# The opening of a two-block transformer kernel: zeros on TensorE, one token half ahead, gate products in two parts

## Chip, cores and metric

One core of one Trainium2 chip. The metric is the device time of one execution in microseconds (µs), the median over several runs. The engines are TensorE (PE, products and transposes; its loads of the stationary operand are PEld), VectorE (DVE), ScalarE (ACT), GpSimd (POOL) and SyncE (SP, which here only issues DMAs).

## The reference

Two transformer blocks run one after the other on 256 tokens of width 1024. What matters here is the start of the first:

```python
u = rms_norm(h, norm_mix_g[l])
z = u @ w_in[l]
qa, ka, va, qk_b, vb, ob, ib, fb, ga, gb = jnp.split(z, IN_SPLITS, axis=-1)
...
i_pre = (ib + b_igate[l].astype(ib.dtype)).transpose(0, 2, 1)
f_pre = (fb + b_fgate[l].astype(fb.dtype)).transpose(0, 2, 1)
hb = mlstm_chunkwise(to_heads(qb, B_HEADS), to_heads(kb_, B_HEADS), to_heads(vb, B_HEADS), i_pre, f_pre)
```

The columns `ib` and `fb` of the input projection are the eight gates (four heads, two each) of a gated recurrence. After the mixers comes a feed-forward layer; the second block has two layers of feed-forward, attention, feed-forward.

## The kernel before

The 256 tokens are two halves, t = 0 and 1, of 128. A half lies in `h[t]` as 128 rows by 1024. For a projection it is turned over by eight transposes on PE (`flip`, L158, each against the identity in `cst`, four to a bank) and multiplied by the gains of the norm on DVE (`uf`, L385); the row's own factor 1/rms (`row_rstd`: a square with sum on ACT, `ms` on DVE, a power on POOL) is multiplied in later.

Each operand is then split in two parts of a four-byte format that PE takes at a quick pace (`fp32r`): a cast on ACT (`uh`, `wh`, L224) and the remainder on DVE (`ul`, `wl`, L225). A weight product is three products, wh·uh, wl·uh and wh·ul, each 128 by 128 by 512 columns (`mm3`, on L153). The weights stream through SP in pieces of 1 MB (`raw`, three buffers; the very first piece is loaded and split in halves), and a new piece is only issued when a buffer comes free.

What runs in which order on PE is written out by a small planner, `Order`: tasks yield either a wait in planned microseconds or events that have a due time, each PE instruction advances the planner's clock, and a task whose time has come puts its PE work there. The other engines' instructions are ordered by a scheduler from the data dependencies and the order of writing.

The opening is `first_mix`. `boundary` turns a half and splits it (planned waits 0 and 2.0 for the two halves). `lin_both` (L326) does the first 48 weight products, for two pieces and both halves. `recurrence` does the eight gate columns by `gate_mm`: 16 full-precision products of `wg` with `uf` (`uf,wg`, 8 by 128 columns, each two rows in the trace), both halves, then bias and arithmetic (`gT`, `gz`, `logf`). `constants` loads `c1`, `masks` and `mlg` and casts the masks (`caus`, `mlm`). `second_params` does small arithmetic for the second block (`pi`, `pf`, `ang`, `nt`, `trig`) whenever DVE has room.

Of the kernel before, what the change touches and what calls it, by code (L numbers as in the profile page):

```python
# [9 lines left out]
FR = mybir.dt.float32r  # L10
BF16 = mybir.dt.bfloat16
# [106 lines left out]
def kernel(  # L118
# [15 lines left out]
    nc = tc.nc  # L134
# [11 lines left out]
    def bank():  # L146
        return psg.tile([128, 512], F32, tag="g", name="bank")
# [4 lines left out]
    def mm(out, lhsT, rhs, start, stop):  # L152
        pe.matmul(out=out, lhsT=lhsT, rhs=rhs, start=start, stop=stop)  # L153
        n = rhs.free_size()
        side.now += n / 2400 if rhs.dtype != F32 else max(n, 128) / 600
# [20 lines left out]
    gc = base.tile([128, G_N], F32, name="gc")  # L176
    nc.scalar.dma_start(out=cst, in_=consts)
    nc.scalar.dma_start(out=gc, in_=cols)
    for t in range(2):
        for c in range(2):  # L180
            nc.sync.dma_start(out=h[t][:, 512 * c:512 * c + 512], in_=x[128 * t:128 * t + 128, 512 * c:512 * c + 512])
    ident = cst[:, C_ID:C_ID + 128]
    mhalf = base.tile([128, 16], F32, name="mhalf")
    pool.memset(mhalf, -0.5)
# [3 lines left out]
    def row_bcast(tile_, lo, n):  # L188
        nc.sync.dma_start(out=tile_, in_=rows[0:1, lo:lo + n].to_broadcast([128, n]))
# [19 lines left out]
    def load_to(n):  # L209
        while stream["load"] < min(n, NP):  # L210
            i = stream["load"]
            if i in kept:
                r = kept[i][0].tile([128, 2048], F32, tag="tx", bufs=2, name="rawx")
            else:
                r = wp.tile([128, 2048], F32, tag="raw", bufs=RAW_BUFS, name="raw")
            n_dma = 2 if i == 0 else 1
            for q in range(n_dma):
                w = 2048 // n_dma
                nc.sync.dma_start(out=r[:, w * q:w * q + w], in_=weights[piece_at.get(i, i), :, w * q:w * q + w])
            raws[i] = r  # L220
            stream["load"] += 1

    def split(hi, lo, src):
        c = act.copy(out=hi, in_=src)  # L224
        dve.tensor_tensor(out=lo, in0=src, in1=hi.bitcast(F32), op=ALU.subtract)  # L225
        return c
# [102 lines left out]
    def lin_both(us, pieces):  # L329

        accs = [bank() for _ in us]
        for a, i in enumerate(pieces):
            for m in range(2):
                for (uh, ul, ready), acc in zip(us, accs):
                    side.until(*ready)
                    wh, wl = half(i, m, 512)
                    for kk in range(2):
                        k = 4 * a + 2 * m + kk
                        mm3(acc, uh[:, k], ul[:, k], wh[:, kk], wl[:, kk], k == 0, k == 4 * len(pieces) - 1)
        return accs  # L340
# [33 lines left out]
    def put_T(u, k0, n, src, gains=None, gain1=None, keep=None):  # L374

        uh, ul, _ = u
        b = trbank()
        for i in range(n):
            flip(b[:, 128 * i:128 * i + 128], src[:, 128 * i:128 * i + 128])
        b3 = b.rearrange("p (k n) -> p k n", n=128)[:, 0:n]  # L380
        hi, lo = uh[:, k0:k0 + n], ul[:, k0:k0 + n]
        if gains is not None:
            s = tmp.tile([128, 4, 128], F32, tag="uf", bufs=4, name="uf") if keep is None else keep[:, k0:k0 + n]
            full[id(u[2]), k0] = s
            dve.tensor_tensor(out=s, in0=b3, op=ALU.mult,  # L385
                              in1=gains.unsqueeze(2).to_broadcast([128, n, 128]))
            split(hi, lo, s)
        elif gain1 is not None:
            act.activation(out=hi, in_=b3, func=AF.Copy, scale=gain1)
            dve.scalar_tensor_tensor(out=lo, in0=b3, scalar=gain1, in1=hi.bitcast(F32),  # L390
                                     op0=ALU.mult, op1=ALU.subtract)
        else:
            split(hi, lo, b3)

    def boundary(t, src, gains, wait=1.4, keep=None, after=None):

        u = new_u(t)
        ev = Ready()
        u[2].append(ev)

        def task():
            yield wait
            with crit():
                for c in range(2):
                    put_T(u, 4 * c, 4, src[:, 512 * c:512 * c + 512], gains=gains[:, 4 * c:4 * c + 4], keep=keep)
            side.ready(ev, 1.3)
            if after is not None:
                after()

        side.spawn(task())  # L410
        return u

    def gcol(lo):
        return gc[:, lo:lo + 8]
# [279 lines left out]
    def first_mix(p0):  # L694
        with tc.tile_pool(name="mix1", bufs=1, reuse_waits="tile") as mix:
            def big(name, shape=(128, 1024), dt=F32):
                return mix.tile(list(shape), dt, tag="c", bufs=C_BUFS, name=name)

            wg = mix.tile([128, 8, 8], F32, name="wg")
            nc.scalar.dma_start(out=wg, in_=w_gates)  # L700
            gbias = mix.tile([128, 8], F32, name="gbias")
            row_bcast(gbias, R_GATE, 8)
            identb = mix.tile([128, 128], BF16, name="identb")
# [3 lines left out]
            mlg = mix.tile([128, 512], F32, name="mlg")  # L707
            oh = mix.tile([128, 4, 128], F32, name="oh")

            def constants():  # L710
                nc.sync.dma_start(out=c1, in_=consts1[:, 0:512])
                masks = big("masks", (128, 256))
                nc.sync.dma_start(out=masks, in_=consts1[:, D_CAUS:D_CAUS + 256])
                row_bcast(mlg, R_MLG, 512)
                dve.tensor_copy(out=identb, in_=ident)
                dve.tensor_copy(out=caus, in_=masks[:, 0:128])
                dve.tensor_copy(out=mlm, in_=masks[:, 128:256])
                for i in range(4):
                    dve.tensor_copy(out=oh[0:4, i], in_=ident[0:4, i:i + 1].to_broadcast([4, 128]))

# [7 lines left out]
            u, r, rh = [], [], []  # L728
            gT = mix.tile([128, 256], F32, tag="th", bufs=2, name="gT")
            gz = mix.tile([128, 2, 8], F32, name="gz")  # L730
            uf = []
            for t in range(2):
                uf.append(big("uf", (128, 8, 128)))
                u.append(boundary(t, h[t], gcol(G_MIX1), 0.0 if t == 0 else 2.0, uf[t]))

            def gate_mm(t):
                gb = bank()
                for k in range(8):
                    mm(gb[0:8, 0:128], wg[:, k], uf[t][:, k], k == 0, k == 7)
                dve.tensor_copy(out=gT[0:8, 128 * t:128 * t + 128], in_=gb[0:8, 0:128])  # L740

            def gates0():
# [134 lines left out]
            def recurrence():  # L877
                for t in range(2):
                    yield u[t][2]
                    gate_mm(t)  # L880
                    r.append(row_rstd(h[t]))
                    rh.append(scaled(r[t], 0.5))
                yield 5.93
                constants()
                gates0()
                yield 0.69
                gates1()
                yield 13.34
                gates2()
                yield 0.83  # L890
                gates3()
                yield 1.87
                gates4()
                for hd in range(5):
                    if hd < 4:
                        yield [gates_ready, cv_ready[0, hd], cv_ready[1, hd]]
                        ml_scores(hd)
                        yield 2.92
                    if hd == 0:
                        yield V1_ready  # L900
                    if hd:
                        ml_out(hd - 1)
                for t in range(2):
                    yield [gob_ready[t]]
                    ml_norm(t)
                    yield 6.39
                    put_T(yT[t], 4, 4, yb[0][:, t])
                    side.ready(y_ready[t][2], 1.81)

            side.spawn(recurrence())  # L910


# [47 lines left out]
            def ev_conv(w):  # L960
                zr = [Ready(), Ready()]

                def convs():
                    yield zr
                    for bl in range(4):
                        conv(w, bl)
                        yield 7.62

                side.spawn(convs())

                def f(t, acc):
                    z = tmp.tile([128, 512], F32, tag="z", name="z")
                    act.activation(out=z, in_=acc, func=AF.Copy, scale=r[t])
                    if t == 0:
                        pool.memset(zT[w][:, :, 0:3], 0.0)

                    def task():
                        yield 1.18
                        act.copy(out=zT[w][:, :, 3 + 128 * t:131 + 128 * t], in_=flip4(z))
                        side.ready(zr[t], 0.57)  # L980

                    side.spawn(task())
                return f
# [654 lines left out]
```

## Time and profile before

| | |
|---|---|
| median of 3 runs | 1374.95 µs (1374.17 to 1375.53) |
| the profiled execution | 1374.35 µs |
| its span on the core | 1372.6 µs |
| PE busy | 1347.2 µs (98%) |
| DVE busy | 1106.1 µs (81%) |
| ACT busy | 853.4 µs (62%) |
| POOL busy | 90.4 µs (7%) |
| PE, first instruction | 3.99 µs from the span's start |
| PE, first weight product | 12.30 µs |

A profile is of one execution. Its span begins with the first instruction that the profiler records; the execution's own time is 1.75 µs longer. Times in the rows below are from the span's start. Busy PE is pipelined: the length of a row overlaps that of the next, so its pace is read from the distance between starts.

### The profile page before, as it was taken

The numbers are of one execution on the slowest core, as the hardware profiler recorded it, in microseconds if no ns is written. First come the engines' busy times: TensorE is split into PE (matmuls) and PEld (weight loads), VectorE is DVE, ScalarE is ACT, GpSimd is POOL, SyncE is SP. The second block draws the span as 40 slices with busy tenths as digits, with TensorE's granted clock in tenths as the row PEclk, the third lists the DMA queues.
The fourth block names the chain that finished last, engine by engine and source line by source line (L and its number), as shares of the span: only waits on it lengthen the run. The fifth ranks groups of instructions, "written<-read, shape, count | busy, mean of one in ns | idle before, by whom it ended". The sixth has DMA issues, their size and how long they took to land.

```text
span 1372.6 us, 17475 instructions
## 1 busy us (share of the span) xinstructions
PE 1347.2 (98%) x6418; PEld 1094.7 (80%) x6418; DVE 1106.1 (81%) x1624; ACT 853.4 (62%) x1327; POOL 90.4 (7%) x89
## 2 busy tenths in 40 slices
PE   8999999999999999999999999999999989999998
PEld 7777888888888888877788888888888767788887
DVE  8866579888789889767689888898897787698884
ACT  6656546665576666568666566666675658566662
POOL 0000000000010000022000000000010211000000
PEclk9999999999999999999999999999999989999999
DMA  8434564976577767463358766677675522567762
GB/s 304 155 115 152 194 227 154 307 237 192 186 255 222 219 254 230 169 216 128 106 211 281 225 229 215 251 220 219 261 215 180 184 99 98 189 196 260 268 188 88
DMA packets 41397, 278.00 MB, mean 203 GB/s; under 512 B 5216, under 2 KB 6240, under 8 KB 8544
## 3 DMA queue, kind: packets, MB, share of 16 engines
q1 hardware_dynamic: 35568, 243.09, 48.6%
q0 software_dynamic: 4320, 31.46, 11.3%
q10 hardware_dynamic: 1424, 2.34, 0.6%
q8 instruction: 50, 0.82, 0.2%
q14 instruction: 35, 0.29, 0.1%
HBM read 244.37 MB, written 1.05 MB: 179 GB/s over the span
## 4 chain that ended last, share of the span: by engine, by line
PE 90%; DVE 6%; POOL 1%; ACT 1%; issue 1%; DMA 0%; DVEq 0%; POOLq 0%; ACTq 0%
PE bank L153 85%; PE trbank L158 5%; DVE wl L225 2%; POOL fac L344 1%; DVE nm L654 1%; DVE ms L1156 0%; DVE z L1160 0%; DVE p L666 0%; ACT wh L224 0%; DVE p L652 0%; ACT p L656 0%; DMA cst<-in_consts_dram 0%; DVE z L1218 0%; DVE z L1220 0%; DVE h L1490 0%
## 5 line engine op out<-in xcount | busy, mean ns | idle before, releaser
L225 DVE TENSOR_TENSOR wl<-raw,wh 128x1024 fp32r<-128x1024 f32 (+1 forms) x548 | 522.0, 978 | 82.9 <-ACT wh L224 76.5
L224 ACT CAST wh<-raw 128x1024 fp32r<-128x1024 f32 (+1 forms) x548 | 454.9, 856 | 126.2 <-PE bank L153 118.4
L153 PE MATMUL bank<-wh,uh 128*128 128x512 f32 x948 | 383.1, 404 | 0.0
L153 PE MATMUL bank<-wh,ul 128*128 128x512 f32 x948 | 373.3, 394 | 0.5 <-DVE ul L225 0.5
L153 PE MATMUL bank<-wl,uh 128*128 128x512 f32 x948 | 372.8, 393 | 0.0
L153 PEld LDWEIGHTS bank<-wh,ul 128*128 128x128 f32 x948 | 179.0, 189 | 40.7 <-DVE ul L225 1.2
L153 PEld LDWEIGHTS bank<-wh,uh 128*128 128x128 f32 x948 | 179.3, 189 | 38.0 <-issue 2.0
L153 PEld LDWEIGHTS bank<-wl,uh 128*128 128x128 f32 x948 | 179.5, 189 | 35.0 <-DVE wl L225 0.3
L153 PE MATMUL bank<-wh,hh 128*128 128x512 f32 x440 | 174.3, 396 | 0.0
L153 PE MATMUL bank<-wl,hh 128*128 128x512 f32 x440 | 172.1, 391 | 0.3 <-DVE wl L225 0.3
L153 PE MATMUL bank<-wh,hl 128*128 128x512 f32 x440 | 172.2, 391 | 0.0
L224 ACT CAST wh<-tn 128x1024 fp32r<-128x1024 f32 x60 | 63.2, 1053 | 100.6 <-PE bank L153 54.4
L225 DVE TENSOR_TENSOR wl<-tn,wh 128x1024 fp32r<-128x1024 f32 x60 | 73.3, 1222 | 39.5 <-ACT wh L224 39.1
L153 PEld LDWEIGHTS bank<-wh,hl 128*128 128x128 f32 x440 | 82.6, 188 | 18.1
L153 PEld LDWEIGHTS bank<-wl,hh 128*128 128x128 f32 x440 | 82.7, 188 | 17.9 <-DVE wl L225 0.8
L153 PEld LDWEIGHTS bank<-wh,hh 128*128 128x128 f32 x440 | 82.7, 188 | 17.0
L153 PE MATMUL bank<-wh,sh 128*128 128x512 f32 x240 | 93.7, 390 | 0.0
L153 PE MATMUL bank<-wl,sh 128*128 128x512 f32 x240 | 93.7, 390 | 0.0
L153 PE MATMUL bank<-wh,sl 128*128 128x512 f32 x240 | 93.6, 390 | 0.0
L224 ACT CAST hh<-trbank 128x512 fp32r<-128x512 f32 (+1 forms) x60 | 33.0, 551 | 62.8 <-PE trbank L158 58.9
L225 DVE TENSOR_TENSOR wl<-rawx,wh 128x1024 fp32r<-128x1024 f32 x60 | 71.6, 1217 | 0.0
L224 ACT CAST wh<-rawx 128x1024 fp32r<-128x1024 f32 x60 | 63.0, 1054 | 13.3 <-PE bank L153 10.8
(248 smaller groups left out, 1533.3 us busy)
## 6 DMA issues: line engine op xcount, KB each, us to landing
raw<-in_weights_dram SPq DMA_DIRECT2D x196, 1024.0 KB, 5.0
rawx<-in_weights_dram SPq DMA_DIRECT2D x30, 1024.0 KB, 8.9
rawx<-rawx POOLq DMA_DIRECT2D x15, 1024.0 KB, 7.8
tn<-raw POOLq DMA_DIRECT2D x15, 1024.0 KB, 7.6
mem<-in_mem_dram ACTq DMA_DIRECT2D x4, 512.0 KB, 3.5
Tb<-in_rel_dram SPq DMA_DIRECT2D x3, 512.0 KB, 5.7
h<-in_x_dram SPq DMA_DIRECT2D x4, 256.0 KB, 3.8
raw<-in_weights_dram SPq DMA_DIRECT2D x2, 512.0 KB, 5.5
```

The source lines that it names most:

```text
L153: pe.matmul(out=out, lhsT=lhsT, rhs=rhs, start=start, stop=stop)
L158: pe.transpose(out=out, in_=in_, identity=ident if identity is None else identity)
L224: c = act.copy(out=hi, in_=src)
L225: dve.tensor_tensor(out=lo, in0=src, in1=hi.bitcast(F32), op=ALU.subtract)
L344: pool.tensor_tensor(out=dst, in0=src, in1=mhalf[:, 0:n], op=ALU.pow)
L654: dve.tensor_reduce(out=nm, in_=s, axis=AX.X, op=ALU.max, negate=True)
```

## The change

Zeros (seven products of 512 columns ahead of the first transposes, twelve behind) go onto PE. The first half of x is loaded ahead of the first weights, the second half behind the first half piece. `lin_both` does a whole piece for the first token half and then for the second, where it had changed over in mid-piece. The weight casts are ordered behind the first half's own casts. The gate products take the two-part operands: `wg` is split into `wgh` and `wgl`, and 3 × 8 products a half replace 8, placed 2.5 planned microseconds behind their operands. Loading the constants is split from using them, and two planned waits are longer.

```diff
+    load_x(0)
...
+                if i == 0 and q == 0:
+                    load_x(1)
...
-            for m in range(2):
-                for (uh, ul, ready), acc in zip(us, accs):
-                    side.until(*ready)
+            for (uh, ul, ready), acc in zip(us, accs):
+                side.until(*ready)
+                for m in range(2):
                     wh, wl = half(i, m, 512)
...
-                    put_T(u, 4 * c, 4, src[:, 512 * c:512 * c + 512], gains=gains[:, 4 * c:4 * c + 4], keep=keep)
+                    cast = put_T(u, 4 * c, 4, src[:, 512 * c:512 * c + 512], gains=gains[:, 4 * c:4 * c + 4], keep=keep)
+            if order[0] is None:
+
+                order[0] = cast
...
+            zeros = mix.tile([128, 512], BF16, name="zeros")
+            dve.memset(zeros, 0.0)
+
+            def idle_products(n):
+                b = bank()
+                for i in range(n):
+                    pe.matmul(out=b, lhsT=zeros[:, 0:128], rhs=zeros, start=True, stop=True)
+
...
-            uf = []
+            idle_products(7)
             for t in range(2):
-                uf.append(big("uf", (128, 8, 128)))
-                u.append(boundary(t, h[t], gcol(G_MIX1), 0.0 if t == 0 else 2.0, uf[t]))
+                u.append(boundary(t, h[t], gcol(G_MIX1), 0.0 if t == 0 else 3.4))
+
+            def filler():
+
+                yield 0.05
+                idle_products(12)
 
             def gate_mm(t):
                 gb = bank()
+                if t == 0:
+                    split(wgh, wgl, wg)
+                uh, ul, _ = u[t]
                 for k in range(8):
-                    mm(gb[0:8, 0:128], wg[:, k], uf[t][:, k], k == 0, k == 7)
+                    mm(gb[0:8, 0:128], wgh[:, k], uh[:, k], k == 0, False)
+                    mm(gb[0:8, 0:128], wgh[:, k], ul[:, k], False, False)
+                    mm(gb[0:8, 0:128], wgl[:, k], uh[:, k], False, k == 7)
                 dve.tensor_copy(out=gT[0:8, 128 * t:128 * t + 128], in_=gb[0:8, 0:128])
...
                     yield u[t][2]
+                    yield 2.5
                     gate_mm(t)
...
-                constants()
+                load_constants()
                 gates0()
                 yield 0.69
                 gates1()
+                constants()
...
+            side.spawn(filler())
             side.spawn(recurrence())
...
-                        yield 1.18
+                        yield 2.4
```

What PE gets at the head of the program stands first in the order of before (`h_75` and `h_76` are the two token halves):

```order
L158 MATMUL trbank<-cst,h_75 128x128 x8
L158 MATMUL trbank<-cst,h_76 128x128 x8
L153 MATMUL bank<-uf,wg 8x128 x16
L153 MATMUL bank<-wh,uh 128x512
L153 MATMUL bank<-wl,uh 128x512
L153 MATMUL bank<-wh,ul 128x512
```

and so in the order after the change, from behind the last zeros, with what each row waits for (a number behind an engine's name is only a mark):

```order
L153 MATMUL bank<-wh,uh 128x512 [waits Activation_49]
L153 MATMUL bank<-wl,uh 128x512 [waits DVE_49]
L153 MATMUL bank<-wh,ul 128x512
L158 MATMUL trbank<-cst,h_76 128x128 [waits DMAHW6_49,PE_49]
L158 MATMUL trbank<-cst,h_76 128x128 x3
L158 MATMUL trbank<-cst,h_76 128x128 [waits DMAHW7_49,PE_49]
L158 MATMUL trbank<-cst,h_76 128x128 x3
L153 MATMUL bank<-wh,uh 128x512 [waits Activation_49]
L153 MATMUL bank<-wl,uh 128x512 [waits DVE_49]
```

The transposes of the second half and all gate products moved behind the first weight products.

On DVE, from the last casts of the first half on, the order of before is this:

```order
L225 TENSOR_TENSOR ul<-uf,uh 128x512
L225 TENSOR_TENSOR ul<-uf,uh 128x512 [waits Activation_49]
L740 COPY gT<-bank 8x128 [waits PE_49]
L362 TENSOR_SCALAR rs<-r 128x1 [waits Pool_49]
L354 TENSOR_SCALAR ms<-ss 128x1
L225 TENSOR_TENSOR wl<-raw,wh 128x512 [waits DMAHW0_49,Activation_49]
L740 COPY gT<-bank 8x128 [waits PE_49]
L362 TENSOR_SCALAR rs<-r 128x1 [waits Pool_49]
L225 TENSOR_TENSOR wl<-raw,wh 128x512 [waits Activation_49]
```

After the change the rows from the first weight split on are these:

```order
L230 TENSOR_TENSOR wl<-raw,wh 128x512 [waits DMAHW4_49,Activation_49]
L230 TENSOR_TENSOR wl<-raw,wh 128x512 [waits Activation_49]
L359 TENSOR_SCALAR ms<-ss 128x1
L367 TENSOR_SCALAR rs<-r 128x1 [waits Pool_49]
L359 TENSOR_SCALAR ms<-ss 128x1 [waits Activation_49]
L390 TENSOR_TENSOR uf<-trbank,gc 128x512 [waits PE_49] x2
L230 TENSOR_TENSOR wl<-raw,wh 128x512 [waits DMAHW0_49,Activation_49]
L230 TENSOR_TENSOR ul<-uf,uh 128x512 [waits Activation_49] x2
L230 TENSOR_TENSOR wl<-raw,wh 128x512
```

The gain products of the second half (`uf`) and the wait for POOL (`rs`) stand between the splits of the first piece's two halves, and the gate copies (`gT`) are gone from there.

Further on, in DVE's order after the change, the casts of the masks have moved between the two halves of the fourth piece's split:

```order
L772 COPY gT<-bank 8x128 [waits PE_49]
L367 TENSOR_SCALAR rs<-r 128x1 [waits Pool_49]
L230 TENSOR_TENSOR wl<-raw,wh 128x512 [waits DMAHW4_49,Activation_49]
L230 TENSOR_TENSOR wl<-raw,wh 128x512 [waits Activation_49]
L772 COPY gT<-bank 8x128 [waits PE_49]
L739 CAST caus<-masks 128x128 [waits DMAHW0_49]
L740 CAST mlm<-masks 128x128
L230 TENSOR_TENSOR wl<-raw,wh 128x512 [waits Activation_49] x2
L230 TENSOR_TENSOR wl<-raw,wh 128x512 [waits DMAHW5_49,Activation_49]
L230 TENSOR_TENSOR wl<-raw,wh 128x512 [waits Activation_49]
L779 SCALAR_TENSOR_TENSOR gz<-trbank,r,gbias 128x8 [waits DMAHW3_49,PE_49]
```

Before, `caus` and `mlm` stood 51 rows behind the second `gT`, among the last of the gate arithmetic; the small parameter operations (`pf` to `trig`) that were in between have gone to the boundary of the feed-forward layer.

## Rows read from the trace of the kernel before

**Rows 1.** The page: busy time, share, instructions; the chain by line
```profile
PE 1347.2 (98%) x6418; PEld 1094.7 (80%) x6418; DVE 1106.1 (81%) x1624; ACT 853.4 (62%) x1327; POOL 90.4 (7%) x89
...
PE bank L153 85%; PE trbank L158 5%; DVE wl L225 2%; POOL fac L344 1%; DVE nm L654 1%; DVE ms L1156 0%; DVE z L1160 0%; DVE p L666 0%; ACT wh L224 0%; DVE p L652 0%; ACT p L656 0%; DMA cst<-in_consts_dram 0%; DVE z L1218 0%; DVE z L1220 0%; DVE h L1490 0%
```

**Rows 2.** What PE waited for, 0 to 100: us in total, times, longest
```profile
PE trbank L158 <- DMA cst<-in_consts_dram: 4.0, 1, 4.0
```

**Rows 3.** Timeline of PE, 0 to 25: start us, us, engine, line, operation
```profile
3.99 4.04 PE L158 MATMUL trbank<-cst,h 128*128 128x128 f32 x16 [3.99 <-DMA cst<-in_consts_dram]
7.96 4.42 PE L153 MATMUL bank<-uf,wg 128*8 128x128 f32 x32
12.30 0.50 PE L153 MATMUL bank<-wh,uh 128*128 128x512 f32 x1
...
16.04 0.39 PE L153 MATMUL bank<-wh,uh 128*128 128x512 f32 x1
...
18.09 0.39 PE L153 MATMUL bank<-wh,uh 128*128 128x512 f32 x1
...
24.48 0.39 PE L153 MATMUL bank<-wh,ul 128*128 128x512 f32 x1
```

**Rows 4.** The same in the stretch 8.5 to 9
```profile
8.13 1.27 PE L153 MATMUL bank<-uf,wg 128*8 128x128 f32 x5
```

**Rows 5.** The same in the stretch 11.5 to 12.8
```profile
11.34 1.04 PE L153 MATMUL bank<-uf,wg 128*8 128x128 f32 x8
```

**Rows 6.** The chain of waits, 0 to 30: start us, us, what
```profile
3.99 1.97 PE trbank L158 x8
...
25.56 0.87 PE trbank L158 x8
```

**Rows 7.** Timeline of ACT, 0 to 18
```profile
1.72 0.38 ACTq L700 DMA_DIRECT2D wg<-in_w_gates_dram  x1
...
5.62 0.19 ACT L350 ACTIVATION_READ_ACCUMULATOR junk<-h 128x1 f32 x1
...
10.02 2.23 ACT L224 CAST wh<-raw 128x512 fp32r<-128x512 f32 x4
```

**Rows 8.** DMA issues: KB each, median us from issue to landing
```profile
masks<-in_consts_dram SPq DMA_DIRECT2D x1, 128.0 KB, 5.8
...
wg<-in_w_gates_dram ACTq DMA_DIRECT2D x1, 32.0 KB, 4.4
```

**Rows 9.** Timeline of DVE, 0 to 21
```profile
6.00 0.69 DVE L385 TENSOR_TENSOR uf<-trbank,gc 128x512 f32<-128x512 f32 x1 [0.16 <-PE trbank L158]
...
12.68 1.87 DVE L225 TENSOR_TENSOR wl<-raw,wh 128x512 fp32r<-128x512 f32 x3
...
20.47 0.35 DVE L747 SCALAR_TENSOR_TENSOR gz<-trbank,r,gbias 128x8 f32<-128x8 f32 x2
```

**Rows 10.** Timeline of PE, 83 to 87 (128-column products of bf16)
```profile
83.93 0.28 PE L153 MATMUL bank<-caus,identb 128*128 128x128 bf16 x2
```

**Rows 11.** Timeline of PE, 44.5 to 48
```profile
46.39 0.23 PE L153 MATMUL bank<-mlm,identb 128*128 128x128 bf16 x1
```

**Rows 12.** Timeline of DVE, 21 to 34
```profile
24.65 0.19 DVE L1127 TENSOR_SCALAR nt<-nt 128x64 f32<-128x64 f32 x1
...
29.38 0.22 DVE L716 CAST caus<-masks 128x128 bf16<-128x128 f32 x1
...
30.59 0.16 DVE L771 SCALAR_TENSOR_TENSOR logf<-gz,pp 128x8 f32<-128x8 f32 x1
```

**Rows 13.** Timeline of SP, 0 to 30
```profile
21.44 0.42 SPq L713 DMA_DIRECT2D masks<-in_consts_dram  x1
```

**Rows 14.** DVE by stretch: busy us, granted clock, DMA share, GB/s
```profile
15.00:20.00 5.00, 4.90 (x12) 1.00 0.88 290
```

**Rows 15.** Timeline of DVE, 199 to 212
```profile
204.80 0.69 DVE L1077 SCALAR_TENSOR_TENSOR h<-bank,h 128x512 f32<-128x512 f32 x1 [2.82 <-PE bank L153]
```

**Rows 16.** What PE waited for, 100 to 1373
```profile
PE trbank L158 <- DVE p L1255: 3.8, 1, 3.8
```

## What the change will do: the prediction

> **What bounds the kernel now.** Times are µs from the span's start. I read the page first: PE is busy for 98% of the span and carries 85% + 5% of the chain on its two lines, the products (L153) and the transposes (L158) [rows 1]. So what counts is work that PE is given, or waits that PE gets, and hardly what the other engines do. Then I read what PE waited for: once in the first 100 µs, 4.0 for the constants in front of its first transpose [rows 2]. The timeline of PE gives the order of that opening: 16 transposes from 3.99, the gate products from 7.96, the first weight product at 12.30, and then one weight product after another [rows 3]. From 16.04 to 18.09 lie 9 of them, .228 each. The 51st starts at 24.48 and so ends at 24.71; the two gate transposes lie before it [rows 3].
>
> The pace of the opening is worth a look. In the middle of the gate products five rows take 1.27, so .21 to .25 lie between starts, by what is allowed for the length of the last; at the end eight take 1.04, in the same way .11 [rows 4, 5]. The eight transposes of a token half take 1.97 there and .87 later [rows 6]. PE's opening runs at half the later pace, which I read as the lower of its two clock levels (1.2 and 2.4 GHz).
>
> So the kernel's opening is 12.3 µs in which PE does no weight product, and everything behind it is a row of PE work without a hole. A change here is worth what it moves a fixed place in that row, and I take the end of the 51st weight product, 24.71.
>
> **The change part by part.** *An earlier first product.* The first token half no longer waits for the second. ACT's square of the first half ends at 5.81 [rows 7]; the gate weights, issued at 1.72 and 4.4 to landing, are there at 6.1 [rows 7, 8], so their short cast (new) ends at about 6.4. Two casts of u at .56 each (four casts of that size take 2.23 [rows 7]) end at 7.5 and the two of the first weight half at 8.6. DVE follows with the differences at .6 each (three take 1.87 [rows 9]): the first weight half is split by 8.8 and 9.4. On PE eight transposes end at 5.96 [rows 6], then come twelve products of zeros, the first at the half pace (.45, twice .228), the rest at .228: 6.0 + .45 + 11 × .228 = 8.95. The first weight product starts at about 8.95 in place of 12.30.
>
> *What comes right behind it.* Six weight products (1.37) end at 10.3, the second half's eight transposes (.87 at the full pace [rows 6]) at 11.2. The weights' next half then has to be split. On DVE the order puts two gain products for the second token half (uf) ahead of that: the first can start after four transposes, at about 10.75, the second ends at about 12.05 (.69 and a pitch of .6 [rows 9]), the split at 12.7. PE has only one product to run meanwhile, and stands for about 1.4 µs. I take 12.8 as the time when it runs on, with 7 of the 51 products done. From below it is 12.3 (ACT had cast the whole piece at 12.25 before [rows 7], the third of four .55 sooner, and .6 for a split); from above 13.3, one more split.
>
> *The gate products.* Before, 16 products (32 rows) lay ahead of 12.30, in time that PE spent waiting anyway. Now there are 48, all behind 12.8, in between weight products. No row of before has the two-part format at 128 columns. From below: two bf16 products of 128 columns take .28, a lone one .23, so .05 lies between starts [rows 10, 11]; a quarter of .228 is .057, and I put the lower end at .056. From above: .11, a row of the same 128 columns by 8 in the four-byte format [rows 5]. I take .08, between them, since this format runs at the quick pace at 512 columns but each product here loads a stationary operand of its own. 48 × .08 = 3.84 (2.7 to 5.3).
>
> The Trainium skill, "TensorE: Matmul & The Clock Gate", section "Back-to-back issue gap", gives about 81 ns for each pair of load and product at 128 columns; by that the term would be 3.9.
>
> *The sum of the opening.* From 12.8: 44 products × .228 = 10.0 and the gate products 3.84, so the 51st ends at 26.65. The two gate transposes, which lay ahead of it, now stand right behind it: .3, taken from the eight of .87 with some room for the change of bank. PE has done at 26.95 what it had done at 24.71: +2.2.
>
> *The masks.* Before, DVE used masks at 29.38 [rows 12], long after they had landed (issued at 21.44, 5.8 to landing [rows 8, 13], so 27.2). Now the two casts of masks stand behind the second gate copy, between the two halves of a weight piece's split. DVE gets there at about 21 and stands until the landing, 5 to 6 µs. Behind it wait the rest of that piece, all later ones, and the gate arithmetic (gz was at 20.47 [rows 9], now about 28.5). DVE has had hardly a free moment there, 4.90 of 5.00 [rows 14], but it also loses some 19 small parameter operations (each about .19 [rows 12], .13 between starts), 2.5 µs. So it falls behind by up to 3. PE needs the delayed half (of the fourth piece) 15 products and eight transposes after 26.95, at 31.2; DVE has it by 29. The gate chain took DVE from 20.47 to 30.75 (logf) [rows 9, 12], so it would end near 39; PE uses its result behind the 114th weight product, which by 12.8 + 107 × .228 + 3.84, with 16 transposes and the two of the gates, is near 43. That covers it by 4; without the cover the price is up to 2.5. I take .3.
>
> *The feed-forward boundary.* The small parameter operations now stand around the residual add (h) that started at 204.80 after 2.82 idle on DVE [rows 15]. Some 12 of them come before its second part, about 2 µs, so they fit into that idle time unless the positions, now loaded just ahead, are late; ACT also has a table load more. Nothing to 1.7; I take .5.
>
> *Free parts.* The earlier load of x and the split of load and use of the constants cost nothing that PE sees, since SP and the queue feed PE only through the splits above; the later convolution task moves a wait that PE does not have.
>
> Together 2.2 + .3 + .5 = +3.0 on the profiled execution's 1374.35, 1377.35. The median of the runs shown is 1374.95, .60 above it; with the same distance, **about 1378.0**.
>
> **The rivals.** *A, the gate products are cheap.* At .056 the term is 2.7, the opening +1.1, and with the masks and the boundary hidden, as the covers above allow, the kernel ends at 1374.95 + 1.1 to 1.9, 1376.0 to 1376.9. For it: the format's 512-column products take .228, one column in .44 ns, and the bf16 row has 128 columns at .05. Against it: 48 of them alternate with 48 loads. This would not be slower by more than .2%; it decides from a price of about .074 down.
>
> *B, 128 columns are slow in this format.* A four-byte gate product of before is two rows of .11; if a two-part product of so few columns got no better than that whole product, .22, the 48 take 10.5 and the sum is +9.6: 1384.6. For it: no product of this format here has fewer than 512 columns. Against it: it always shows one row, not two.
>
> *C, zeros do not raise the clock.* Twelve at .45 end at 11.4 instead of 8.95; all behind them on DVE moves by 2.4 (transposes, uf, split): 1380.4. For it: nothing in the profile shows zeros on PE, and before, PE kept the low level until well into the gate products, at 9 µs, after 5 µs of work [rows 3, 4]. Against it: it now starts work before 3.99, without a wait for a DMA.
>
> The section "What's actually happening" of the same page of the Trainium skill makes the clock rise with sustained activity of the array; by that the zeros serve, and C falls.
>
> *D, DVE's wait for masks reaches PE*, with the boundary's 1.7: +2.2 + 2.5 + 1.7, 1381.3. It decides if the gate chain ends over 4 µs later than I have it.
>
> *E, faster.* PE has waits elsewhere, the largest 3.8 [rows 16]. That one ends with DVE and lies where the order is the same, so I see no mechanism that would take 2.75 from it or the others; in the opening even at .056 and with the run-on at 12.3 the sum is +.6.
>
> **How the numbers follow.** .2% is 2.75 µs, about what a measurement of this kernel can tell from no change. The forecast (1377.0 to 1379.0) has a chance of .42, A .30, B .08, C .08, D .05, E .07. The range reaches down to 1374.0, below A's best, and up to 1382.0, above C and D: left out are B and most of E, under .2. Faster is E, .07. Slower (above 1377.7) are three quarters of the forecast, B, C and D: .32 + .21 = .53. The rest is the same, .40.
>
> **What would show it.** In the profile after: zeros on PE from about 1 and again from 6 at .23; the first weight product near 9; eight transposes of .87 behind the sixth; a wait of PE for a split (wl) of 1 to 2 ending near 12.8; 24 gate rows in about 1.9, twice; the 51st weight product's end near 27. DVE should stand for the masks until about 27 with no new wait of PE for the gate chain, and at the boundary (now near 208) PE should lose under 1. The prediction is wrong if the gate rows are .056 or .2 apart, if the wait near 12 is missing, if the first weight product is not before 10.5, or if a later wait of PE grows or vanishes by more than 1 µs.

## The result, and the profile after

The changed kernel takes 1382.28 µs (median of 4 runs, 1380.87 to 1383.85), the kernel before 1374.56 (4 runs, 1373.41 to 1375.53): a ratio of 1.0059, 95% interval 1.0045 to 1.0074. It is slower by 7.7 µs, where 3.0 were forecast. The profiled execution took 1382.28, and its span is 7.9 longer than that of before.

The page of the changed kernel, the span and the busy times:

```profile
span 1380.5 us, 17547 instructions
...
PE 1352.9 (98%) x6453; PEld 1097.1 (79%) x6453; DVE 1106.7 (80%) x1626; ACT 854.5 (62%) x1329; POOL 89.9 (7%) x89
```

Busy PE has grown by 5.7, its share is the same [rows 1]. So PE has more to do or does it more slowly, and where, the timeline of the opening tells. First ACT (start, length, operation, and in brackets the idle time before it and what ended it):

```profile
1.73 0.38 ACTq L717 DMA_DIRECT2D wg<-in_w_gates_dram  x1
...
7.79 0.24 ACT L229 CAST wgh<-wg 128x64 fp32r<-128x64 f32 x1 [1.91 <-DMA wg<-in_w_gates_dram]
7.94 1.13 ACT L229 CAST uh<-uf 128x512 fp32r<-128x512 f32 x2
```

The gate weights (wg) are asked for at 1.73 as before, but land at 7.77, after 6.04, where it was 4.4 [rows 8]. Their small cast (wgh) stands first in ACT's order, and ACT waits 1.91 for it. The casts of u stand behind: their input was ready at 5.7 to 6.3, and they start at 7.94. PE shows what comes of it:

```profile
4.15 1.19 PE L158 MATMUL trbank<-cst,h 128*128 128x128 f32 x8
5.18 2.75 PE L714 MATMUL bank<-zeros 128*128 128x512 bf16 x12
9.64 0.51 PE L153 MATMUL bank<-wh,uh 128*128 128x512 f32 x1 [1.71 <-ACT wh L229]
10.54 0.50 PE L153 MATMUL bank<-wl,uh 128*128 128x512 f32 x1 [0.39 <-DVE wl L230]
10.87 0.45 PE L153 MATMUL bank<-wh,ul 128*128 128x512 f32 x1
11.12 0.63 PE L153 MATMUL bank<-wh,uh 128*128 128x512 f32 x1
11.54 0.63 PE L153 MATMUL bank<-wl,uh 128*128 128x512 f32 x1
...
12.40 1.91 PE L158 MATMUL trbank<-cst,h 128*128 128x128 f32 x8
```

The twelve zeros behind the transposes end at 7.93, and the first weight product starts at 9.64. That is .7 later than I had it, after 1.71 of idle time, and the second waits another .39. Then the pace changes: .25 lie between the third product and the fourth, and .43 from there on; the eight transposes, ahead of the product at 13.96, take 1.6 in place of .87 [rows 6]. The view of stretches gives PE's busy time and, behind it, the granted clock, the DMA share and GB/s:

```profile
11.00:16.00 5.00, 4.00 (x15) 0.66 0.59 243
```

The granted clock fell: a mean of .66 from 11 to 16 (and .51 from 11 to 14, the level of 1.2 GHz). All of this is upstream of DVE's two gain products for the second token half (uf), and they stand ahead of the split (wl) that PE needs next:

```profile
13.49 0.69 DVE L390 TENSOR_TENSOR uf<-trbank,gc 128x512 f32<-128x512 f32 x1 [1.38 <-PE trbank L158]
...
14.95 0.68 DVE L230 TENSOR_TENSOR wl<-raw,wh 128x512 fp32r<-128x512 f32 x1
```

So PE goes on like this:

```profile
13.96 0.73 PE L153 MATMUL bank<-wh,uh 128*128 128x512 f32 x1
15.69 0.50 PE L153 MATMUL bank<-wl,uh 128*128 128x512 f32 x1 [1.00 <-DVE wl L230]
...
16.26 0.22 PE L153 MATMUL bank<-uh,wgh 128*8 128x128 f32 x1
...
17.69 0.45 PE L153 MATMUL bank<-wh,uh 128*128 128x512 f32 x1
```

PE runs on at 15.69, with 7 of the 51 products done, where I had 12.8. The gate products are the one thing that came out cheaper: 24 from 16.26 to 17.69, .060 each, 2.9 for the 48.

Further on PE has waits that were not there before [rows 2]. The view of what PE waited for in the first 100 µs (in total, times, longest):

```profile
...
PE trbank L158 <- DVE at L813: 1.0, 1, 1.0
PE trbank L158 <- DVE gz L779: 0.9, 1, 0.9
PE trbank L158 <- DVE z L1041: 0.6, 1, 0.6
PE trbank L158 <- DVE Mrow L820: 0.3, 1, 0.3
```

These four, 2.8 in all, are the ones behind the opening: gz, at and Mrow come between 30 and 55, and z at 88.84. DVE's timeline has the origin of the first three:

```profile
29.68 0.23 DVE L739 CAST caus<-masks 128x128 bf16<-128x128 f32 x1 [5.00 <-DMA masks<-in_consts_dram]
```

DVE stands for 5.00 in front of the first cast of the masks. PE's timeline around the gate transposes (28.95), and some of the transposes of z behind them:

```profile
28.95 0.29 PE L158 MATMUL trbank<-cst,gT 8*128 8x8 f32 x2
...
31.34 0.60 PE L158 MATMUL trbank<-cst,z 128*128 128x128 f32 x4
32.87 0.63 PE L158 MATMUL trbank<-cst,z 128*128 128x128 f32 x4 [0.92 <-DVE gz L779]
...
88.84 0.66 PE L158 MATMUL trbank<-cst,z 128*128 128x128 f32 x4 [0.61 <-DVE z L1041]
```

The second four of z need a bank that the gate arithmetic (gz) has not yet read, since gz stands behind the masks on DVE. At the gate transposes' end, 29.24, PE is 4.5 later than at 24.71 before. The idle time of the four waits adds 2.8, but they cost more. The profile counts idle time from the modelled end of the row before, and a row that does not wait starts earlier than that. By the distance between starts, the z of 88.84 begins 1.01 behind the product before it, and in the kernel before such a row begins .23 behind (80.66 and 80.89), so this wait costs .8 and not .6. In the same way gz costs 1.1, at 1.2 and Mrow .3. Together the four cost 3.4, and with the 4.5 that makes 7.9. A fixed place behind all of them, the products of qkT, is here in the kernel before:

```profile
109.60 0.70 PE L153 MATMUL bank<-qkT 64*128 64x256 f32 x4
```

and here in the changed kernel:

```profile
117.59 0.70 PE L153 MATMUL bank<-qkT 64*128 64x256 f32 x4
```

They are 8.0 later, and the end of the span is 7.9 later. So everything is lost before 110 µs, and the feed-forward boundary costs nothing.

### The profile page after: what moved, and what is told of

It reads as the page before. It is cut to its first block, busy times and chain, and to the rows that moved or that the text cites. A ratio compares the mean times of both kernels' runs of the same rounds, so it can differ in the third digit from the quotient of the medians.

```text
span 1380.5 us, 17547 instructions
## 1 busy us (share of the span) xinstructions
PE 1352.9 (98%) x6453; PEld 1097.1 (79%) x6453; DVE 1106.7 (80%) x1626; ACT 854.5 (62%) x1329; POOL 89.9 (7%) x89
## 3 DMA queue, kind: packets, MB, share of 16 engines
q0 software_dynamic: 4320, 31.46, 11.2%
## 4 chain that ended last, share of the span: by engine, by line
PE 87%; DVE 8%; ACT 1%; POOL 1%; issue 1%; DMA 1%; ACTq 0%; SPq 0%; DVEq 0%; POOLq 0%
PE bank L153 83%; PE trbank L158 4%; DVE wl L230 3%; POOL fac L349 1%; ACT wh L229 1%; DVE nm L662 1%; DMA masks<-in_consts_dram 0%; DMA wg<-in_w_gates_dram 0%; DVE cv L850 0%; DVE z L1195 0%; DVE p L674 0%; DVE p L660 0%; DVE ms L1191 0%; DVE ul L230 0%; DVE z L1253 0%
```

## The experiments

All were timed against the kernel before, on the same chip as their neighbours. The kernel before had medians of 1374.5 to 1375.3 in these groups, and its single runs lie within 1371.5 to 1377.7. The span is that of the one profiled execution.

| kernel | median µs | ratio to before, 95% interval | span µs |
|---|---|---|---|
| changed kernel | 1382.28 | 1.0059 (1.0045 to 1.0074) | 1380.5 |
| the same again (e11) | 1380.62 | 1.0041 (1.0026 to 1.0056) | 1379.4 |
| e1: masks later | 1378.32 | 1.0034 (1.0021 to 1.0047) | 1376.5 |
| e2: gate cast later | 1377.21 | 1.0024 (1.0012 to 1.0036) | 1376.3 |
| e3: both | 1375.38 | 1.0009 (1.0000 to 1.0019) | 1373.8 |
| e4: 20 zeros | 1379.74 | 1.0044 (1.0031 to 1.0056) | 1378.5 |
| e5: x first | 1380.77 | 1.0038 (1.0024 to 1.0053) | 1375.7 |
| e6: e3 without zeros | 1378.54 | 1.0028 (1.0017 to 1.0039) | 1377.8 |
| e7: before with 7 zeros | 1375.04 | 1.0005 (.9995 to 1.0014) | 1374.5 |
| e8: e3, transposes first | 1377.27 | 1.0013 (1.0004 to 1.0022) | 1375.6 |
| e9: e3, 6 of 48 gate products | 1373.55 | .9995 (.9986 to 1.0003) | 1372.4 |
| e10: e3, convolution wait back | 1375.31 | 1.0006 (.9994 to 1.0018) | 1375.9 |
| e12: e10, transposes first | 1374.71 | 1.0000 (.9991 to 1.0009) | 1375.3 |

**e1, the masks.** The theory was that DVE's stand for the masks is one of two separate losses.

```diff
-                dve.tensor_copy(out=caus, in_=masks[0][:, 0:128])
-                dve.tensor_copy(out=mlm, in_=masks[0][:, 128:256])
+                behind(dve.tensor_copy(out=caus, in_=masks[0][:, 0:128]), last_gate[0])
+                behind(dve.tensor_copy(out=mlm, in_=masks[0][:, 128:256]), last_gate[0])
```

`behind` only orders two instructions of one engine; `last_gate` is the instruction that writes `logf`.

> The changed kernel with one thing different: the two casts of the masks on DVE are ordered behind the last of the gate arithmetic (logf), where they stood before the change. Theory (DVE stood 5.0 us for the masks and the gate arithmetic behind it reached PE late): PE's four waits between 30 and 60 us (gz .9, at 1.0, z .6, Mrow .3, together 2.8) go, the opening up to the 51st weight product stays as it is, 1379.5 us. Rival (the gate chain is late because the whole opening is): the waits stay or only move, 1381.5 to 1382.3.

What PE waited for in the first 100 µs:

```profile
...
PE trbank L158 <- DVE z L1051: 0.6, 1, 0.6
...
```

The rows left out are waits of the opening. The waits for gz, at and Mrow are gone, 2.2 in all; that for z stays, so the masks do not cause it. The time fell by 4.0 against the first runs of the changed kernel, by 2.3 against its second ones (e11). In e1's profile PE runs on at 14.32, as in e11 (14.20), so e11 is the fairer measure: the theory, less z.

**e2, the gate weights' cast, and e3, both.**

```diff
-                    split(wgh, wgl, wg)
+                    behind(split(wgh, wgl, wg), w_casts[1])
```

> The changed kernel with one thing different: on ACT the cast of the gate weights is ordered behind the first two weight casts, not ahead of the casts of u. Theory (ACT stood 1.9 us for the gate weights' landing, so PE ran out of zeros, stood, and ran the next six products and eight transposes at half the pace): the casts of u start near 6, the first weight product starts at 8 to 8.5, no half pace, PE runs on after the wait for the second split at 12.7 to 13.3 in place of 15.7, about -2.7, 1379.6 us. Rival (PE then waits just as long for the second half piece, and falls to half pace in that wait): under 1 us saved, 1381.3 or more.

PE's timeline in e2:

```profile
8.91 0.58 PE L153 MATMUL bank<-wh,uh 128*128 128x512 f32 x1
9.34 0.39 PE L153 MATMUL bank<-wl,uh 128*128 128x512 f32 x1
...
10.50 1.03 PE L158 MATMUL trbank<-cst,h 128*128 128x128 f32 x8
11.29 0.47 PE L153 MATMUL bank<-wh,uh 128*128 128x512 f32 x1
11.96 0.50 PE L153 MATMUL bank<-wl,uh 128*128 128x512 f32 x1 [0.19 <-DVE wl L230]
```

The first weight product starts at 8.91; from the second to the transposes five starts take 1.16, .23 each, and the transposes take .8 up to the seventh product at 11.29. Up to there the opening is what I had forecast, and in e11, whose pace held as well, the seventh product is at 12.41: the late gate weights cost 1.1 by then. PE runs on at 11.96, .8 sooner than forecast, and that is not the cast's doing alone. In this build the scheduler has also put DVE's split of the second half piece ahead of the second half's gain products:

```profile
11.21 0.69 DVE L230 TENSOR_TENSOR wl<-raw,wh 128x512 fp32r<-128x512 f32 x1
11.82 1.28 DVE L399 TENSOR_TENSOR uf<-trbank,gc 128x512 f32<-128x512 f32 x2
```

In the changed kernel, e1, e6 and e11 the gain products come first; in e2, e3, e4, e5, e9 and e10 the split does. From the seventh product to the eighth PE takes .67 here and 1.79 in e11, so the turn may be worth as much as the cast. The time is 3.4 to 5.1 lower, more than the 2.7 of the theory, and no run has the cast's share of it alone.

> Both of the above in one kernel. Theory (two separate losses): the savings add, -5.5, 1376.8 us, which is still about 2 above the kernel before, the price of 48 gate products that lie in the open (48 x .06 = 2.9) and of the wait for the second split, less the earlier start. Rival (the two are one loss, whichever comes first on the path): no more than the better of the two, 1379.5. Second rival (nothing is left but the gain of the early start): below 1374.6.

The median is 1375.38, between the theory's 1376.8 and the second rival. The two savings add nearly in full (5.2 against 2.3 + 3.4, by the second runs of the changed kernel). The profiles agree: at the products of qkT e11, e1, e2 and e3 are 6.5, 4.1, 3.8 and 2.1 behind the kernel before, so 4.4 is saved against 2.4 + 2.7. What is left against before, +.9 in the medians, has an interval from nothing to 2.6. The prediction's sum had +2.2 for the opening; with gate products at .060 it would have been +1.3.

**e4, more zeros.**

```diff
-                idle_products(12)
+                idle_products(20)
```

> The changed kernel with 20 products of zeros in place of 12 behind the first transposes, so that PE works until about 9.8 us. Theory (the idle 1.7 us ahead of the first weight product cost the clock): the first six weight products start .23 apart, not .43, and the eight transposes take .9, not 1.7; PE runs on at 14.3 to 14.6 in place of 15.7, -1.2 us, 1381.0. Rival (the half pace has to do with what these products read or wait for, not with the idle time): pace as in the changed kernel, and no gain or .2 lost, 1382.3 to 1382.5.

PE's timeline in e4:

```profile
10.36 0.51 PE L153 MATMUL bank<-wh,uh 128*128 128x512 f32 x1 [0.79 <-ACT wh L229]
...
11.82 0.39 PE L153 MATMUL bank<-wh,uh 128*128 128x512 f32 x1
12.05 0.39 PE L153 MATMUL bank<-wl,uh 128*128 128x512 f32 x1
...
14.32 0.50 PE L153 MATMUL bank<-wl,uh 128*128 128x512 f32 x1 [0.55 <-DVE wl L230]
```

.23 lie between products, and from the first to the seventh PE takes 2.94 (to 13.30) where the changed kernel took 4.32. That PE runs on at 14.32 in place of 15.69 is in part DVE's turned order, which this build has too. The time is 2.5 below the first runs of the changed kernel and .9 below its second, whose pace held as well. So the profile shows a pace that held, but not that the added zeros held it: in e11 and e5 it held without them, after 1.2 and 1.9 of idle time.

**e5, the order of the loads.** One line of the change undone: `load_x(1)` stands ahead of the weights again.

> The changed kernel with one part undone: both halves of x are loaded ahead of the first weights again. Theory (the first weight half, issued ahead of the second half of x and without a wait, shares the DMA engines with the gate weights and so they land at 7.8 instead of 6.1): gate weights near 6.2, the casts of u from 6.4, the first weight product near 9.3 since the weights now come later; PE runs on at 13 to 14 in place of 15.7, 1380.0 to 1381.0 us. Rival (the gate weights land late whatever goes ahead of them, or the later weights eat the gain): first product at 9.6 or later, 1381.5 to 1382.5.

ACT's timeline in e5:

```profile
6.08 0.24 ACT L228 CAST wgh<-wg 128x64 fp32r<-128x64 f32 x1 [0.26 <-DMA wg<-in_w_gates_dram]
...
10.01 1.14 ACT L228 CAST wh<-raw 128x512 fp32r<-128x512 f32 x2 [2.56 <-DMA raw<-in_weights_dram]
```

The gate weights land at 6.08, 1.7 sooner. The first weights land at 10.0 instead, so the first weight product starts at 10.68, which is the rival's. PE runs on at 13.88 and the median is 1380.77, both in the theory's ranges. The theory is right about the load that delays the gate weights; a gain is not shown, since the changed kernel has the same time the second time (e11).

**e6, the zeros' worth.** e3, with `idle_products(7)` and the task with the twelve taken out.

> The kernel with both casts moved back, without any product of zeros. Theory (the zeros are what brings PE to full pace for the first products): transposes take 1.9, PE stands until about 8.7, the first six weight products start .43 apart and the second eight transposes take 1.7; PE runs on about 1.5 to 2 later than with zeros (12.3), 1376.9 to 1377.4 us. Rival (the waits for loads and splits set the time in the opening, not PE's pace): within .5 of the kernel with zeros, 1375.4 to 1375.9.

PE's timeline in e6:

```profile
9.12 0.79 PE L153 MATMUL bank<-wh,uh 128*128 128x512 f32 x1 [3.38 <-ACT wh L229]
...
10.86 0.63 PE L153 MATMUL bank<-wh,uh 128*128 128x512 f32 x1
11.29 0.63 PE L153 MATMUL bank<-wl,uh 128*128 128x512 f32 x1
...
15.44 0.50 PE L153 MATMUL bank<-wl,uh 128*128 128x512 f32 x1 [0.96 <-DVE wl L230]
```

Its view of stretches:

```profile
11.00:16.00 5.00, 4.04 (x15) 1.00 0.63 258
```

Without zeros PE is slow, .43 between products, and runs on at 15.44, in e3 at 12.29. The medians differ by 3.2, their ratios to before by 2.6: the theory, and more than I had. But not all of it is the zeros': here DVE has the gain products (13.24) ahead of the split (14.70) again, in e3 behind it. At the seventh product, ahead of that split, e6 is 2.2 behind e3 (13.71 and 11.51), near the theory's 1.5 to 2. So the zeros do bring PE to its pace, once the operands come in time, and here they are worth about 2.

**e7, seven zeros in the kernel before**, ahead of its first transposes, and nothing else.

> The kernel before with one part of the change alone: seven products of zeros ahead of the first transposes. Theory (the opening's pace is PE's): the 16 transposes and 32 gate rows run at the full pace from about 5 us on, the first weight product starts at 11.2 in place of 12.30, 1373.4 us. Rival (the first weight split on DVE, done at 11.8, sets the start whatever PE's pace): 11.8 to 12.0 and 1374.0. Third (the zeros change nothing or hold PE up): 1374.5 or more.

PE's timeline in e7:

```profile
9.14 0.63 PE L158 MATMUL trbank<-cst,h 128*128 128x128 f32 x4 [2.26 <-DMA h<-in_x_dram]
```

The time lies in the third's range, but none of the three mechanisms was put to the test. In this build the first weights no longer wait for the constants before they are issued (2.58, before 3.96), the second half of x lands only at 9.0, and the first weight product starts at 14.95. That the weights take the DMA engines from x is likely, and argued only. The median is still that of before, and the two spans, 1374.5 here and 1372.6 there, differ by less than single executions of one kernel do. As a test of the zeros alone it is inconclusive.

**e8, e10 and e12, two planned waits back.** In e8 `3.4` is `2.0` again, in e10 `2.4` is `1.18` again, in e12 both, all on top of e3.

> The kernel with both casts moved back and the second half's boundary planned at 2.0 again, as before the change, so that its eight transposes lie between the zeros and the first weight product, where PE stood .7 for the first weights. Theory (the transposes fill that wait, and DVE can do the second half's gain products while it waits for ACT): -.5 to -1.0 against the 1375.4 of the kernel with only the casts moved, 1374.4 to 1374.9. Rival (DVE is then later with the splits that PE waits for next): no gain, 1375.4 to 1376.2.

> The kernel with both casts moved back, and the planned wait of the convolution task at 1.18 again, as before the change. Theory (the longer planned wait is what makes PE wait .6 for z): that wait goes, -.6, 1374.8 us. Rival (the wait comes from the boundary's later end and stays, or another takes its place): 1375.2 to 1375.8.

> The kernel with both casts moved back, with the convolution task's wait at 1.18 and the second half's boundary at 2.0, both as before the change. Theory (with z's wait and the wait for Mrow gone, the transposes ahead of the first weights give back what they cover): 1374.2 to 1374.8 us. Rival (the gate chain is still late for Mrow, 1.3): 1376 or more.

In e8 PE runs into a wait for the gate chain, in the view of what it waited for in the first 100 µs:

```profile
PE trbank L158 <- DVE Mrow L830: 1.3, 1, 1.3
```

Neither side had that: the waits for splits, which the rival named, are no longer than in e3 (.4 and .5), and 1377.27 lies above both ranges. In e10 the wait for z goes, so the longer planned wait made it, and another comes at the feed-forward boundary, in DVE's timeline and in what PE waited for between 195 and 225:

```profile
201.01 0.17 DVE L1149 CAST pf<-pi 128x2 f32<-128x2 int32 x1 [7.24 <-DMA pi<-in_positions_dram]
```

```profile
PE trbank L158 <- DVE h L1122: 1.6, 1, 1.6
```

DVE stood 7.24 for the positions, with the residual add behind them. It is the mechanism that I had for that boundary, near its upper end (1.6 of 1.7); in the changed kernel it cost nothing. e10 is where its rival has it. e12 lies in its theory's range, and that is the time of before, no less. Its profile does not bear the theory out, though: the waits for z and Mrow are gone, but the transposes put ahead of the first weights stand themselves, for the second half of x.

```profile
PE trbank L158 <- DMA h<-in_x_dram: 0.6, 1, 0.6
```

At the products of qkT e12 is 2.4 behind before, e3 2.1 and e10 1.6. So as far as that one execution shows, its number came out by luck. The intervals of e3, e8, e10 and e12 overlap, and which of them is fastest is not shown.

**e9, what the gate products cost.** e3, with the loop over eight blocks cut to its first; this leaves out seven eighths of the gates' sum.

```diff
                 for k in range(8):
-                    mm(gb[0:8, 0:128], wgh[:, k], uh[:, k], k == 0, False)
+                    if k == 0:
+                        mm(gb[0:8, 0:128], wgh[:, k], uh[:, k], True, False)
...
+                    else:
+                        side.now += 3 * 128 / 2400
```

> The kernel with both casts moved back, and of the 48 gate products only 6 done (one block of 128 of the eight; this leaves out most of the gates' sum), in the same two places of PE's order. Theory (the gate products lie in the open on PE): 42 x .06 = 2.5 off the kernel's 1375.4, 1372.9 us. Rival (the first 24 cover PE's wait for the second split of the first piece, done at 14.03 by DVE, so that a wait of .7 to 1 takes their place): 1.5 to 1.8 off, 1373.6 to 1373.9. Second rival (they are hidden altogether): 1375.2 or more.

PE's timeline in e9, at the place of the first 24:

```profile
13.56 0.51 PE L153 MATMUL bank<-wl,uh 128*128 128x512 f32 x1 [0.59 <-DVE wl L230]
```

The time is 1.83 off, at the edge of the first rival. The medians alone, each good to about 1.2, do not decide against the theory's 2.5, but the trace does: where the first 24 gate products were, .59 of waiting for the split is left. Of 2.5 some seven tenths lie in the open.

**e11, the changed kernel again.**

> The changed kernel as it is, once more, to see which of its waits come again in another execution. Theory (the late gate weights and DVE's stand for the masks come in every execution): gate weights at 7.5 to 8, gz, at, z and Mrow waits of 2.5 to 3 in all, 1381.5 to 1383 us; the fall of PE's pace ahead of the sixth product comes again. Rival (the half pace after about 11 us is a chance of that one profile): .23 between these products, 1380.5 to 1382.

The stretches of PE in e11, and its timeline:

```profile
11.00:16.00 5.00, 3.69 (x36) 1.00 0.53 219
```

```profile
9.46 0.50 PE L153 MATMUL bank<-wh,uh 128*128 128x512 f32 x1 [1.24 <-ACT wh L229]
...
12.41 0.48 PE L153 MATMUL bank<-wh,uh 128*128 128x512 f32 x1
14.20 0.50 PE L153 MATMUL bank<-wl,uh 128*128 128x512 f32 x1 [1.31 <-DVE wl L230]
```

The gate weights were late again (7.60), and the first product at 9.46; the four waits behind came again, 2.6. But the clock held (1.00 from 11 to 16), as the rival had it, and PE runs on at 14.20. The fall is a matter of the single execution, and worth 1.5 there. The median, 1380.62, is 1.7 below the first one.

## Why the prediction was wrong

The direction was right. Of the 7.7 the sum had 3.0, and the time lay outside the range by .3; the same kernel's second runs (1380.62) lie inside it, so that much may be chance. The errors in the sum are not. In the profiles the kernel lost 7.9. Of the 4.9 that the sum lacks, the opening has 2.3, the masks 2.3 and the wait for z .8, less the .5 that the boundary did not take. By the prediction's own steps:

*An earlier first product: a step that failed, by one input.* I took the gate weights' landing at 6.1 from an issue-to-landing time of before, in a step that moves 512 KB of weights ahead of the second half of x. e5 shows that this move is what takes the landing from 6.1 to 7.8. I had written that the loads' order costs nothing that PE sees. The cast behind that landing is the head of ACT's row, so u was cast 1.5 later than I had it (7.94, not 6.4), and in the one profile the clock fell on top. PE ran on at 15.69, not 12.8: +2.9. Up to the seventh product, forecast for 11.2 and measured at 13.96, it is 2.8: 1.2 by the late weights (e11 has it at 12.41, e2 at 11.29) and 1.6 by the pace.

*The gate products: right in mechanism, too dear.* They took .060 each and not .08, so 2.9 and not 3.84. The rule of the Trainium skill that I set beside it ("TensorE: Matmul & The Clock Gate", section "Back-to-back issue gap", 81 ns for a pair at 128 columns) was further off than the lower row, .056. Some seven tenths of the 2.5 that e9 takes away lie in the open. That the 16 products of before lay in time that PE spent waiting is a wrong reading: PE shows no wait there [rows 2, 3]. The sum does not use it.

*The masks: a step that failed, by its cover.* The stand had the length that I had for it, 5.0, but ended at 29.7 and not at 27: the masks were issued at 23.14, before at 21.44 [rows 13]. I covered it by looking at one reader, the product that takes logf: it is at 46.62, and logf was done at 39.1, so that cover held. But PE also needs the bank from which gz is read, and later at and Mrow, which queue on DVE behind the convolution's work. Each was late: 2.2 of idle time, 2.6 by the distance between starts, where I had .3. Rival D had DVE's wait reach PE, with a chance of .05, but by a gate chain that ends over 4 later than forecast; the chain ended as forecast, and the wait reached PE by the bank.

*The convolution's planned wait: wrong.* I had it among the free parts. It makes PE wait .6 for z (e1, e10).

*The boundary: in its range*, nothing where I had .5, and 1.6 in e10.

*The zeros: right.* Rival C did not come; without them the seventh product is 2.2 later (e6). The trace agrees with the rule of the Trainium skill that stood beside rival C (the same page, section "What's actually happening"), that sustained work raises the clock: the seven zeros ahead of the transposes start .42 apart, the twelve behind .23. In one execution of those profiled the pace fell again after PE had stood.

With both misplaced casts moved the kernel is at 1.0009 of before, about what the prediction's opening gives with the cheap gate products (+1.3). In part that is luck: e3 runs on at 12.29 and not at 12.8 by DVE's turned order, and its wait for z was in no sum of mine. No run that does all of the work beats before. The zeros win about 2, and the gate products cost 1.8 (e9). What the early weights and the late second half win or cost by themselves is not shown; e5, e8 and e12 take back one or the other without a clear gain.

What stays open is why the clock fell in one execution after 1.7 and .4 of idle time and not in another (e11, after 1.2 and .4; e5, after 1.9 and .2), and what the cast of the gate weights costs without the turn in DVE's order.

## What to carry to other kernels

When a transfer is moved forward, go through every small transfer that was in flight beside it, and read which engine has the consumer of each at the head of its row. When an instruction that waits for a load moves up in an engine's row, look at everything behind it that another engine needs, buffers to be freed included, and not only at the result that the row is named for. Filling an idle TensorE with products of zeros was worth about 2 µs here, where the operands were there soon after the zeros ended. And before a run's saving is put down to its one edit, compare the order of every engine: a scheduler can move other instructions with it, as it moved DVE's split in e2, e3 and e4, and back in e6.

## What was not expected of the hardware

A load of 32 KB took 6.0 to land with 512 KB of weights issued just ahead of the rest of x, and 4.3 with the rest of x ahead of these weights (e5). It took 5.9 to 6.9 in all eleven profiles with the first order, and 4.3 to 4.5 in the three with the second (before, e5, e7). Products of this four-byte format with 128 columns and a stationary operand of 8 start .060 apart, hardly more than bf16 products of 128 columns (.05) [rows 10, 11]. In e6 PE's first products run at half the pace from 9 to 14 while that profile gives a granted clock of 1.00 for the stretch from 11 to 16; in the changed kernel the same pace goes with .66. So in these profiles the granted clock shows a fall, and not that the pace has not yet risen; the kernel before has 1.00 from 5 to 9 as well, at half the pace [rows 4].
